# The adaLN matmuls of layer 0 with the weights as the stationary side, and a copy of scan states on VectorE

## The chip, the cores and the metric

The kernel runs on one core of a Trainium2 chip. The metric is the device time of one launch in microseconds, as the median of several runs. In the text PE is TensorE (the matmuls), DVE is VectorE, ACT is ScalarE, POOL is GpSimd, and SP is the engine whose queue issues most of the DMA transfers.

## The reference

One inference step of a hybrid backbone with two layers. 128 prompt tokens and 1024 latent tokens, 1152 in all, have 1024 channels. Each layer normalizes x, modulates it, feeds the result `h` to three branches (an S5 state-space scan, a Fourier mixing, an attention), gates and merges them, and adds the result to x. Cut to what matters here:

```python
def adaln(cvec, w, b):                       # w: (1024, 3072), b: (3072,)
    m = jax.nn.silu(cvec) @ w + b
    shift, scale, gate = jnp.split(m[:, None, :], 3, axis=-1)
    return shift, scale, gate

# in mixer_layer, with cvec = c_ctx for the prompt and c for the latents:
    shift, scale, gate = adaln(cvec, ada_w, ada_b)
    h = rmsnorm(x, norm_g) * (1.0 + scale) + shift
    a_in, a_gate, f_in, f_gate, q, k, v, c_gate = jnp.split(h @ w_in, SPLITS, axis=-1)
    # S5: hs[t] = a_bar * hs[t-1] + b_bar @ u[t], forwards and backwards;
    # the prompt's final states of both directions are an output (new_state_ssm)
```

There are thus only two conditioning vectors, and the product `silu(cvec) @ w` has two rows. All is computed in fp32.

## The kernel before

The channels lie on the 128 partitions in 8 blocks (`KD`), the 1152 tokens in the free dimension, in three groups j = 0, 1, 2 of 384. The dense products (`dense`, line 269) hold a 128x128 block of the weights as the stationary side and 384 tokens as the moving side. Weights and `h` are split in a rounded part and a rest (`whi`, `wlo`; `hh`, `hl`), and three matmuls give one product. ACT rounds the weights, POOL subtracts, and ACT mostly evicts a finished block from PSUM (`jo`) with two buffers `pd` in turn.

The head of the program, in `run` (line 1541), comes ahead of layer 0:

- `setup` (line 176) loads the identity, the first x tile, the small vectors (`fvst`, 128 rows of 128 numbers) and constants on SP's queue, transposes the vectors on PE into columns (`fv`) and computes the silu of both conditioning vectors (`silc`).
- `x_gen` (line 398) takes nine x tiles of 128 tokens: ACT and DVE sum the squares, PE transposes eight blocks of 128x128, ACT and DVE evict them into `A1` (in the profile `A`).
- `ada_gen` (line 306) computes the shift and scale of layer 0. The conditioning columns are the stationary side (4 columns), the weights move, 512 columns at a time. 16 units of 512 KB are loaded with `ada_load` into four buffers `aw`. Of each unit one half goes as an fp32 matmul, the other is rounded on ACT, subtracted on DVE or POOL and goes as two matmuls. After four units a row of results (`adarow`) is copied by ACT and turned into columns by four matmuls with `sel` as the moving side (`ada_row`).
- `rb_first_gen` computes the row scales of all tokens (DVE, a power on POOL, transposes on PE, a copy by ACT) and x times the scale for j = 0 (`xr0`). `h_first_gen` makes `h` for three j and first k from 0 to 3, then from 4 to 7, with `h_unit` (line 456): one product, an addition on ACT (`hh`), a difference on DVE (`hl`); j = 0 needs them twice, since prompt and latents have different shifts and scales.

In each layer, `scan_gen` (line 706) runs 128 steps of the scan on DVE, four operations each, beside 12 dense blocks. In the first 16 steps it also advances the prompt's states; these steps end with the prompt's final states in column 16 of `H` (in the profile `A`). When the scan has been traced, `finals` (line 727) copies them (`ss_fin`, on ACT), transposes them on PE, copies the results on ACT into a tile of tag `qk_sq` and stores them. Behind the scan the q/k/v work goes on beside two dense blocks; then the pool `gp` of this stage is closed and the next one, with `ssm_out_gen` (line 738, it reads the scanned states), opens.

The order of the instructions of an engine isn't the order of the program. The framework plans it when the program is built, from its own estimates of when an instruction's inputs are ready, and program order as the priority. On the chip each engine then works off its list strictly in that order, and waits at an instruction whose inputs are late, whatever stands behind it. DMA queues are issued in the same way.

Of the kernel before, what the change touches and what calls it, by code (L numbers as in the profile page):

```python
# [9 lines left out]
F = mybir.dt.float32  # L10
R = mybir.dt.float32r
AF = mybir.ActivationFunctionType
OP = mybir.AluOpType
# [10 lines left out]
KD = D // 128  # L24
# [77 lines left out]
class Program:  # L102
# [73 lines left out]
    def setup(self):  # L176
        nc, I = self.nc, self.I
        self.ident = self.sb("ident", [128, 128])
        self.dma(self.ident, I["ident"])
        self.load_x(0, 1)  # L180
        self.identr = self.sb("identr", [128, 128], R)
        nc.gpsimd.dma_start(self.identr, I["ident"])
        self.ones = self.sb("ones", [128, 1])
        nc.vector.memset(self.ones, 1.0)
        self.fold = self.sb("fold", [128, 32])
        for i in range(4):
            nc.vector.tensor_copy(self.fold[32 * i:32 * i + 32], self.ident[32 * i:32 * i + 32, 32 * i:32 * i + 32])
        self.half9 = self.sb("half", [128, 9])
        nc.gpsimd.memset(self.half9, -0.5)
        self.half = self.half9[:, :8]  # L190
        vecs = [("c", I["c"][0], 8), ("c_ctx", I["c_ctx"], 8), ("norm_g", I["norm_g"], 16), ("ada_b", I["ada_b"], 48),
                ("merge_b", I["merge_b"], 48)]
        st = self.sb("fvst", [128, 128], pool=self.xp)
        off = 0
        self.fv = {}
        col = self.sb("fv", [128, 128])
        for nm, ap, k in vecs:
            self.dma(st[off:off + k], ap.rearrange("l (k p) -> (l k) p" if len(ap.shape) == 2 else "(k p) -> k p", p=128))
            n = k // DEPTH
            for l in range(1 if len(ap.shape) == 1 else DEPTH):  # L200
                self.fv[nm, l] = col[:, off + n * l:off + n * l + (n if len(ap.shape) == 2 else k)]
            off += k
        ps = self.pst("pv")
        self.tr(ps[:, :off], st[:off])
        self.act(col[:, :off], ps[:, :off])
        self.mods = {}
        self.sel = self.sb("sel", [4, 2])
        self.dma(self.sel, I["sel"])
        self.silc = self.sb("silc", [128, KD, 4])
        nc.gpsimd.memset(self.silc, 0.0)  # L210
        sc = self.silc[:, :, 0:2]
        self.act(sc[:, :, 0], self.fv["c_ctx", 0], AF.Silu)
        self.act(sc[:, :, 1], self.fv["c", 0], AF.Silu)
        self.sc4 = self.sb("sc4", [128, KD, 4], R)
        self.act(self.sc4[:, :, 0:2], sc)
        self.tt(self.sc4[:, :, 2:4], sc, self.sc4[:, :, 0:2].bitcast(F), OP.subtract)
        self.hmb = []
        for l in range(DEPTH):
            t = self.sb(f"hmb{l}", [128, 24])
            nc.vector.tensor_scalar(t, self.fv["merge_b", l], 0.5, None, op0=OP.mult)  # L220
            self.hmb.append(t)
        self.dmask = self.sb("dmask", [128, 16])
        self.dma(self.dmask, I["dmask"])
        self.xT_d = [self.dp.tile([D, NT], F, name=f"xTd{l}") for l in range(DEPTH)]

    def vec_cols(self, v):
# [76 lines left out]
        self.dma(st, self.I["ada_w"][l, 256 * k:256 * k + 256, 512 * o:512 * o + 512].rearrange("(a p) n -> p a n", p=128))  # L303
        return st

    def ada_gen(self, l, pool, parts, bufs=3, first=False):
        self.ada_alloc(l)
        units = [(o, k) for o in parts for k in range(4)]
        ld = {}
        def load(i):  # L310
            ld[i] = self.ada_load(l, pool, bufs, *units[i])
        for i in range(bufs - 1):
            load(i)
        for i, (o, k) in enumerate(units):
            if i + bufs - 1 < len(units):
                load(i + bufs - 1)
            if i == 0:
                pa = self.ps.tile([128, 3, 512], F, name="pa", tag="pa", bufs=1)
            ps = pa[:, i // 4 % 3]
            st = ld.pop(i)  # L320
            for h in range(2):
                ends = (k == 0 and h == 0, k == 3 and h == 1)
                if first and (h == 0 or i >= 16):
                    self.mm(ps[0:4, :], self.silc[:, 2 * k + h], st[:, h], *ends)
                else:
                    w = self.sb("awr", [128, 2, 512], R, bufs=3 if first else 2, pool=pool)
                    self.act(w[:, 0], st[:, h])
                    self.tt(w[:, 1], st[:, h], w[:, 0].bitcast(F), OP.subtract, e=self.nc.gpsimd if first and i >= 7 else None)
                    self.mm(ps[0:4, :], self.sc4[:, 2 * k + h], w[:, 0], ends[0], False)
                    self.mm(ps[0:4, :], self.sc4[:, 2 * k + h], w[:, 1], False, ends[1])  # L330
                if h == 0:
                    if i > 3 and k == 0:
                        self.ada_row(l, units[i - 1][0], row)
                    yield 2 * 216
            if k == 3:
                row = self.sb("adarow", [4, 512], bufs=1, pool=pool)
                self.act(row, ps[0:4, :])
            if i + 1 == len(units):
                self.ada_row(l, o, row)
            yield 2 * 216  # L340

    def ada_row(self, l, o, row):
        pc = self.pst("pt")
        for b in range(4):
            self.mm(pc[:, 2 * b:2 * b + 2], row[:, 128 * b:128 * b + 128], self.sel)
        self.ada_out(l, o, pc)

    def ada_out(self, l, o, pc):
        mod, A = self.mods[l]["mod"], self.mods[l]["A"]
# [127 lines left out]
                self.h_unit(l, j, k, xT[:, k, 384 * j:384 * j + 384], rb, self.xr_tile())  # L477
                yield 900

    def rb_first_gen(self, xT, ssq):  # L480
        self.tt(ssq[:, 0], ssq[:, 0], ssq[:, 1], OP.add)
        r = self.rstd_cols(ssq[:, 0], 9)
        self.rb = [self.rstd_rows(r[:, 3 * j:3 * j + 3], 3) for j in range(3)]
        self.h_tiles()
        self.xr0 = self.sb("xr0", [128, KD, 384], pool=self.xp)
        for k in range(KD):
            self.tt(self.xr0[:, k], xT[:, k, 0:384], self.rb[0], OP.mult)
            yield 500

    def h_first_gen(self, xT, js, ks):  # L490
        for j in js:
            for k in ks:
                if j == 0:
                    self.h_unit(0, j, k, self.xr0[:, k], None, self.xr_tile())
                else:
                    self.h_unit(0, j, k, xT[:, k, 384 * j:384 * j + 384], self.rb[j], self.xr_tile())
                yield 500

    def rhs_h(self, k, j):
        return self.hh[j][:, k], self.hl[j][:, k]  # L500
# [205 lines left out]
    def scan_gen(self, l):  # L706
        S, H = self.S, self.H
        for k in range(128):
# [13 lines left out]
            self.tt(t1, t1, nxt, OP.add)  # L722
            self.tt(nxt, t1, t2, OP.add)
            yield 800
        self.finals(l)

    def finals(self, l):
        H = self.H
        fin = self.sb("ss_fin", [128, 2, 32], pool=self.gp)
        self.act(fin, H[:, :, :, 16])  # L730
        o = self.sb("qk_sq", [32, 2, 64, 2], pool=self.gp)
        for r in range(2):
            ps = self.pst("pv")
            self.tr(ps[:32, :128], fin[:, r])
            self.act(o[:, :, :, r], ps[:32, :128].rearrange("g (d n) -> g d n", d=2))
        self.dma(self.O[4][0, l].rearrange("d g n r -> g d n r"), o)
# [552 lines left out]
    def layer(self, l, cs):  # L1289
# [140 lines left out]
        with self.spool:  # L1430
# [11 lines left out]
            with self.pool("qp", l):  # L1442
                with self.pool("gp", l, "q"):
                    self.qkt = self.qkv_tables(l)
                    def qkv():
                        yield from self.qkv_gen(l, qs_d, k_d, v_d, (0,))
                        yield from self.qkv_gen(l, qs_d, k_d, v_d, (1,))
                    q = qkv()
                    self.run_some(q, 8)
                    drive((self.scan_gen(l), 103), (self.dense(12), 140))  # L1450
                    drive((q, 78), (self.dense(2), 21))
                with self.pool("gp", l, "o"):
                    drive((self.dense(6), 12*6), (self.ssm_out_gen(l, a_d, y_d), 33), (self.qtail_gen(), QT))
        with self.pool("gp", l, "u"):
# [86 lines left out]
    def run(self):  # L1541
        self.open_ssm(0)
        with ExitStack() as cs:
            self.np_ = cs.enter_context(self.tc.tile_pool(name="np", bufs=1))
            self.xp = cs.enter_context(self.tc.tile_pool(name="xp", bufs=1))
            self.setup()
            self.load_x(1, 9)
            self.xT0 = xT = self.sb("A1", [128, KD, NT])
            ssq = self.sb("ssqt", [128, 2, 9], pool=self.xp)
            ada = self.ada_gen(0, self.xp, (2, 0, 3, 1), 4, True)  # L1550
            next(ada)
            self.run_all(self.x_gen(xT, ssq))
            rb = self.rb_first_gen(xT, ssq)
            head = self.h_first_gen(xT, [0, 1, 2], range(0, 4))
            for i, _ in enumerate(ada):
                if i >= 10:
                    self.run_some(rb if i < 18 else head, 1)
            self.run_all(rb)
            self.run_all(head)
            self.run_all(self.h_first_gen(xT, [0, 1, 2], range(4, 8)))  # L1560
        for l in range(DEPTH):
            for j in range(3):
                self.debug(f"hh{l}", self.hh[j].bitcast(F), (slice(None), slice(None), slice(384 * j, 384 * j + 384)))
# [31 lines left out]
```

## Time and profile before

| | us |
|---|---|
| median of 3 runs | 2754.29 (2752.75 to 2756.11) |
| the profiled execution's own time | 2752.03 |
| its span in the profile | 2750.3 |
| PE busy | 2627.0 (96%) |
| DVE busy | 1826.6 (66%) |
| ACT busy | 1143.5 (42%) |
| POOL busy | 683.4 (25%) |

The span is the time from the first to the last instruction of the profiled execution. Busy times are sums over the instructions of an engine; PE's ends of matmuls are modelled, so that neighbouring matmuls overlap in the rows. Times in rows count from the span's start. PEclk is the granted clock of TensorE, 1.00 for 2.4 GHz and 0.50 for 1.2 GHz.

### The profile page before, as it was taken

The page shows a single profiled execution, that of the slowest core. Times are in us where ns is not written, and L with a number is a line of the kernel's source. Part 1 is how long each engine was busy: PE and PEld are TensorE (multiplying, and loading weights), DVE is VectorE, ACT ScalarE, POOL GpSimd, SP SyncE. Part 2 cuts the span into 40 slices and gives each one's busy share as a digit, 9 for nine tenths or more (in the row PEclk, how much of TensorE's full clock was granted, in tenths as well). Part 3 has the DMA queues.
Part 4 walks back from the last instruction along what each step waited for, and adds up shares of the span by engine and source line. Part 5 has one row for each costly group of instructions (what it writes and reads, how often), then busy time and mean ns, then how long its engine had stood idle before and what let it go on. Part 6 is the DMA issues. An engine that isn't in the chain of part 4 may idle for free. (4 is left out here: it accounts for less than half of the span.)

```text
span 2750.3 us, 44553 instructions
## 1 busy us (share of the span) xinstructions
PE 2627.0 (96%) x16092; PEld 2509.0 (91%) x16092; DVE 1826.6 (66%) x3933; ACT 1143.5 (42%) x2676; POOL 683.4 (25%) x521
## 2 busy tenths in 40 slices
PE   7998999899999999999999899999999999999998
PEld 3898999799999999999989899989989998999998
DVE  6549955856558889866572797577654788891343
ACT  5461145331355565423345322543223655553244
POOL 3241122322321020132343212233222202102223
PEclk9999999999999999999999999999999999999999
DMA  6632223566263345544543222345645334433244
GB/s 223 178 99 84 95 87 110 150 191 207 86 202 114 110 138 153 173 126 114 165 146 93 95 89 84 107 125 160 211 154 174 109 121 150 143 121 98 80 121 149
DMA packets 459997, 366.85 MB, mean 133 GB/s; under 512 B 72953, under 2 KB 432001, under 8 KB 459777
## 3 DMA queue, kind: packets, MB, share of 16 engines
q1 hardware_dynamic: 458480, 359.75, 42.9%
q0 software_dynamic: 1296, 4.26, 0.5%
q8 instruction: 127, 2.08, 0.3%
q14 instruction: 94, 0.76, 0.1%
HBM read 243.52 MB, written 120.39 MB: 132 GB/s over the span
## 5 line engine op out<-in xcount | busy, mean ns | idle before, releaser
L168 PE MATMUL pd<-hh,whi 128*128 128x384 f32 x2496 | 857.1, 344 | 24.0 <-ACT jo L142 20.1
L168 PE MATMUL pd<-hh,wlo 128*128 128x384 f32 x2496 | 844.6, 339 | 3.2 <-POOL wlo L145 3.2
L168 PE MATMUL pd<-hl,whi 128*128 128x384 f32 x2496 | 843.1, 338 | 1.3 <-DVE hl L149 1.3
L145 POOL TENSOR_TENSOR wlo<-wst,whi 128x512 fp32r<-128x512 f32 x312 | 437.9, 1405 | 1525.8 <-ACT whi L142 1404.8
L168 PEld LDWEIGHTS pd<-hh,whi 128*128 128x128 f32 x2496 | 472.5, 189 | 35.0 <-ACT jo L142 22.8
L168 PEld LDWEIGHTS pd<-hh,wlo 128*128 128x128 f32 x2496 | 472.5, 189 | 7.8 <-POOL wlo L145 5.7
L168 PEld LDWEIGHTS pd<-hl,whi 128*128 128x128 f32 x2496 | 473.1, 190 | 3.8 <-DVE hl L149 2.3
L168 PE MATMUL pd<-A,whi 128*128 128x384 f32 x1728 | 458.2, 342 | 8.2 <-ACT jo L142 4.9
L168 PEld LDWEIGHTS pd<-A,whi 128*128 128x128 f32 x1728 | 311.2, 189 | 11.7 <-ACT jo L142 5.6
L142 ACT ACTIVATE whi<-wst 128x512 fp32r<-128x512 f32 x312 | 196.0, 630 | 278.5 <-PE pd L168 190.6
L168 PE MATMUL pd<-A,wlo 128*128 128x384 f32 x864 | 293.9, 340 | 0.0
L1078 DVE TENSOR_REDUCE at_mx<-pa 128x1 f32<-128x1152 f32 x128 | 173.3, 1354 | 16.1 <-PE pa L168 15.7
L168 PE MATMUL pa<-at_K,at_Q 128*128 128x384 f32 x768 | 167.2, 347 | 8.6 <-ACT at_P L142 5.8
L142 ACT ACTIVATE at_PT<-pt 128x384 fp32r<-128x384 f32 (+1 forms) x260 | 114.9, 490 | 144.0 <-PE pt L173 143.6
L142 ACT ACTIVATE at_P<-pa,at_mx 128x1152 f32<-128x1152 f32 x128 | 158.1, 1235 | 20.7 <-DVE at_mx L1078 19.4
L168 PEld LDWEIGHTS pd<-A,wlo 128*128 128x128 f32 x864 | 163.2, 189 | 0.1
L168 PEld LDWEIGHTS pa<-at_K,at_Q 128*128 128x128 f32 x768 | 128.3, 188 | 29.0 <-ACT at_P L142 25.5
L168 PE MATMUL pt<-qkW,hh 128*128 128x384 f32 x576 | 150.7, 343 | 0.0
L168 PE MATMUL pv<-at_PT,at_V 128*128 128x256 f32 x1152 | 148.8, 283 | 0.0
L168 PEld LDWEIGHTS pv<-at_PT,at_V 128*128 128x128 f32 x1152 | 144.7, 191 | 0.8
L142 ACT ACTIVATE jo<-pd 128x384 f32<-128x384 f32 x120 | 58.0, 485 | 198.1 <-PE pd L168 96.5
L145 DVE TENSOR_TENSOR at_PT<-pt,at_PT 128x384 fp32r<-128x384 f32 (+1 forms) x260 | 133.1, 550 | 10.0 <-ACT at_PT L142 7.8
(294 smaller groups left out, 3772.3 us busy)
## 6 DMA issues: line engine op xcount, KB each, us to landing
aw<-in_ada_w_dram SPq DMA_DIRECT2D x48, 512.0 KB, 4.8
wst<-in_merge_w_dram SPq DMA_DIRECT2D x96, 256.0 KB, 3.0
wst<-in_w_in_dram SPq DMA_DIRECT2D x80, 256.0 KB, 2.9
td<-jo SPq DMA_DIRECT2D x96, 192.0 KB, 2.3
jt<-td SPq DMA_DIRECT2D x96, 192.0 KB, 2.8
wst<-in_w_out_dram SPq DMA_DIRECT2D x64, 256.0 KB, 2.9
sgd<-jo SPq DMA_DIRECT2D x72, 192.0 KB, 2.0
jt<-sgd SPq DMA_DIRECT2D x64, 192.0 KB, 2.7
```

Of the source, the lines that this page charges most:

```text
L142: return self.nc.scalar.activation(out, in_, func, **kw)
L145: return (e or self.nc.vector).tensor_tensor(out=out, in0=a, in1=b, op=op)
L168: return self.nc.tensor.matmul(out, w, x, start=first, stop=last, **kw)
L1078: nc.vector.tensor_reduce(out=mx[:, 0:1], in_=src, axis=AX.XY if m3 else AX.X, op=OP.max, negate=True)
```

## The change

Two edits. In the head, the adaLN weights of layer 0 become the stationary side: `ada_first_gen` loads 8 units, each 256 columns of the weights over all 1024 rows, in two transfers of 512 KB into four buffers, and multiplies each 128x128 block with the two conditioning columns. The result is in columns at once. The units come in pairs, the scale and the shift of the same two blocks k. x tiles 3 to 8 are loaded between the first units and transposed between the pairs; row scales are computed for each j alone; `h` of j = 0 is made for two k after each pair, that of j = 1 one pair later, that of j = 2 at the end. The small vectors and two constants are loaded on POOL's queue. `ada_gen`, `ada_row`, `sel` and the split copy `sc4` go; `ada_out` stays for the other parts of adaLN.

In each layer, `finals` is called after the q/k/v work, and its first copy goes to DVE. `keep_in_program_order` makes the planner keep it behind every instruction traced before it on DVE.

```diff
 def setup(self):
-        self.load_x(0, 1)
-        self.identr = self.sb("identr", [128, 128], R)
-        nc.gpsimd.dma_start(self.identr, I["ident"])
+        self.load_x(0, 3)
+        pdma = nc.gpsimd.dma_start
...
-            self.dma(st[off:off + k], ap.rearrange("l (k p) -> (l k) p" if len(ap.shape) == 2 else "(k p) -> k p", p=128))
+            pdma(st[off:off + k], ap.rearrange("l (k p) -> (l k) p" if len(ap.shape) == 2 else "(k p) -> k p", p=128))
...
-        self.dma(self.dmask, I["dmask"])
+        pdma(self.dmask, I["dmask"])
+        self.identr = self.sb("identr", [128, 128], R)
+        pdma(self.identr, I["ident"])
...
+    def ada_first_gen(self, l, pool):
         self.ada_alloc(l)
...
+        mod, A = self.mods[l]["mod"], self.mods[l]["A"]
+        units = [2 * q + 8 * p for q in range(4) for p in (1, 0)]
+        ld = []
+
+        def load(m):
+            st = self.sb("aw", [128, KD, 256], bufs=4, pool=pool)
             for h in range(2):
+                self.dma(st[:, 4 * h:4 * h + 4], self.I["ada_w"][l, 512 * h:512 * h + 512, 128 * m:128 * m + 256].rearrange("(k p) n -> p k n", p=128))
+            ld.append(st)
+
+        for i in range(4):
+            load(units[i])
+            self.load_x(3 + i, 4 + i if i < 3 else 9)
+        pa = self.ps.tile([128, 3, 512], F, name="pa", tag="pa", bufs=1)
+        for i, m in enumerate(units):
+            ps = pa[:, i % 3, 0:4].rearrange("p (m c) -> p m c", c=2)
+            for b in range(2):
+                for k in range(KD):
+                    self.mm(ps[:, b], ld[i][:, k, 128 * b:128 * b + 128], self.silc[:, k], k == 0, k == KD - 1)
+            if i < 4:
+                load(units[i + 4])
+            s = slice(m, m + 2)
+            self.tt(mod[:, s], ps, self.fv["ada_b", l][:, s][:, :, None].to_broadcast([128, 2, 2]), OP.add)
+            if m >= 8:
+                g = slice(m - 8, m - 6)
+                self.stt(A[:, g], mod[:, s], 1.0, self.fv["norm_g", l][:, g][:, :, None].to_broadcast([128, 2, 2]), OP.add, OP.mult)
+            yield i
...
+    def rb_first(self, ssq, j):
+        c = slice(3 * j, 3 * j + 3)
+        self.tt(ssq[:, 0, c], ssq[:, 0, c], ssq[:, 1, c], OP.add)
+        self.rb[j] = self.rstd_rows(self.rstd_cols(ssq[:, 0, c], 3), 3)
...
 scan_gen:
             yield 800
-        self.finals(l)
...
 finals:
-        self.act(fin, H[:, :, :, 16])
+        self.tc.keep_in_program_order(self.nc.vector.tensor_copy(fin, H[:, :, :, 16]))
...
 layer:
                     drive((q, 78), (self.dense(2), 21))
+                    self.finals(l)
...
 run:
+            ada = self.ada_first_gen(0, self.xp)
+            xg = self.x_gen(xT, ssq)
+            self.run_some(xg, 6)
+            self.h_tiles((0,))
+            self.rb_first(ssq, 0)
+            for q in range(4):
+                self.run_some(ada, 2)
+                for k in (2 * q, 2 * q + 1):
+                    self.xr_first(xT, k)
+                    self.h_first(xT, 0, k)
+                if q < 3:
+                    self.run_some(xg, 4)
+                if q == 1:
+                    self.h_tiles((1,))
+                    self.rb_first(ssq, 1)
+                if q == 2:
+                    self.run_all(xg)
+                    self.h_tiles((2,))
+                    self.rb_first(ssq, 2)
+                if q > 0:
+                    for k in (2 * q - 2, 2 * q - 1):
+                        self.h_first(xT, 1, k)
+            for k in (6, 7):
+                self.h_first(xT, 1, k)
+            for k in range(KD):
+                self.h_first(xT, 2, k)
```

`xr_first` and `h_first` hold the bodies of the former loops: x times the row scale for j = 0, and one call of `h_unit`.

## Rows read from the trace of the kernel before

**Rows 1.** The page: the span, part 1, and one group of part 5.

```profile
span 2750.3 us, 44553 instructions
PE 2627.0 (96%) x16092; PEld 2509.0 (91%) x16092; DVE 1826.6 (66%) x3933; ACT 1143.5 (42%) x2676; POOL 683.4 (25%) x521
...
L168 PE MATMUL pd<-hh,whi 128*128 128x384 f32 x2496 | 857.1, 344 | 24.0 <-ACT jo L142 20.1
```

**Rows 2.** Windows of all engines: x tiles, adaLN, first dense blocks.

```profile
core 0: us, PE busy (x) PEld busy (x) DVE busy (x) ACT busy (x) POOL busy (x), PEclk, DMA share, GB/s
8.25:14.15 5.90, 4.09 (x17) 3.35 (x17) 1.85 (x9) 4.90 (x12) 0.00 (x0) 1.00 0.82 292
14.15:24.50 10.35, 8.79 (x56) 6.52 (x56) 7.34 (x22) 9.95 (x23) 0.00 (x0) 1.00 1.04 403
24.50:65.10 40.60, 32.90 (x98) 8.04 (x98) 28.31 (x51) 19.90 (x40) 20.98 (x13) 0.83 0.62 197
65.10:100.00 34.90, 32.52 (x176) 29.25 (x176) 26.49 (x77) 19.12 (x45) 6.48 (x5) 1.00 0.65 183
```

**Rows 3.** Timeline of PE in the head: start, duration, group, idle time before it.

```profile
8.48 1.94 PE L173 MATMUL pt<-ident,hl 128*128 128x128 f32 x8 [8.48 <-DMA dmask<-in_k_dmask_dram]
...
52.80 0.59 PE L168 MATMUL pa<-awr,sc 128*4 128x512 f32 x1 [3.60 <-POOL awr L145]
...
65.16 0.34 PE L168 MATMUL pd<-hh,whi 128*128 128x384 f32 x1
```

**Rows 4.** Timeline of ACT in the scan stage, layer 0 and layer 1.

```profile
223.66 0.32 ACT L142 ACTIVATE ss_fin<-A 128x64 f32<-128x64 f32 x1 [12.25 <-DVE A L145]
...
1565.48 0.32 ACT L142 ACTIVATE ss_fin<-A 128x64 f32<-128x64 f32 x1 [12.25 <-DVE A L145]
```

**Rows 5.** Timeline of PE, the first dense matmul behind each of those copies.

```profile
224.93 0.69 PE L168 MATMUL pd<-hh,whi 128*128 128x384 f32 x1 [7.84 <-ACT jo L142]
...
1566.74 0.69 PE L168 MATMUL pd<-hh,whi 128*128 128x384 f32 x1 [7.83 <-ACT jo L142]
```

**Rows 6.** Windows of all engines after those two matmuls, and just behind.

```profile
224.93:240.00 15.07, 15.07 (x72) 15.07 (x73) 14.24 (x49) 2.46 (x5) 3.48 (x3) 0.81 0.31 99
240.00:255.07 15.07, 15.07 (x89) 15.07 (x88) 14.18 (x53) 3.12 (x6) 2.72 (x2) 1.00 0.29 94
1566.74:1580.00 13.26, 13.26 (x63) 13.26 (x64) 12.57 (x43) 2.47 (x5) 3.52 (x3) 0.80 0.28 90
1580.00:1593.26 13.26, 13.26 (x78) 13.26 (x78) 12.50 (x45) 2.63 (x5) 2.78 (x2) 1.00 0.30 96
```

**Rows 7.** Timeline of DVE, its first instruction after the scan of layer 0.

```profile
369.01 0.17 DVE L871 TENSOR_SCALAR qk_ss<-qk_ss 128x4 f32<-128x4 f32 x1 [10.85 <-ACT qk_j L142]
```

**Rows 8.** DMA issues: queue, count, KB each, median us from issue to landing.

```profile
aw<-in_ada_w_dram SPq DMA_DIRECT2D x48, 512.0 KB, 4.8
...
fn_t<-in_k_dft_l_dram POOLq DMA_DIRECT2D x8, 512.0 KB, 8.1
```

**Rows 9.** PE windows of four sel matmuls: length, busy (x), PEclk, DMA share, GB/s.

```profile
32.57:33.55 0.98, 0.98 (x9) 1.00 0.88 328
55.86:57.65 1.79, 1.79 (x9) 0.50 1.12 330
```

**Rows 10.** Timeline of PE, the sums of squares of layer 1.

```profile
1370.14 0.72 PE L168 MATMUL pv<-ones,ssq 128*128 128x1 f32 x6
```

**Rows 11.** Windows of all engines, 50 to 60 us.

```profile
50.00:55.00 5.00, 1.53 (x3) 0.17 (x3) 2.08 (x5) 1.87 (x5) 3.97 (x2) 0.50 0.13 32
55.00:60.00 5.00, 5.00 (x14) 1.96 (x12) 2.41 (x7) 2.57 (x6) 2.79 (x3) 0.50 1.01 283
```

**Rows 12.** The instructions of tile fn_t: POOL's DMA issues, ns min/median/max.

```profile
L993 POOL DMA_DIRECT2D fn_t<-in_k_dft_l_dram x8: 537/545/647, 670.6 to 2013.1; - x8
```

**Rows 13.** Timeline of DVE and of POOL in the head.

```profile
36.57 8.16 DVE L145 TENSOR_TENSOR xr<-A,rb 128x384 f32<-128x384 f32 x8 [1.46 <-ACT rb L142]
...
25.54 2.13 POOL L145 TENSOR_TENSOR rs<-ms,half 128x9 f32<-128x9 f32 x1 [23.36 <-DVE ms L432]
```

More of the change, by code (lines that the diff above doesn't have):

```diff
@@ L206, in setup @@
         self.mods = {}
[L207 to L211, printed above, removed]
+        self.silc = self.sb("silc", [128, KD, 2])
+        sc = self.silc
         self.act(sc[:, :, 0], self.fv["c_ctx", 0], AF.Silu)
         self.act(sc[:, :, 1], self.fv["c", 0], AF.Silu)
-        self.sc4 = self.sb("sc4", [128, KD, 4], R)
-        self.act(self.sc4[:, :, 0:2], sc)
-        self.tt(self.sc4[:, :, 2:4], sc, self.sc4[:, :, 0:2].bitcast(F), OP.subtract)
         self.hmb = []
@@ L304, in ada_load @@
         return st
-    def ada_gen(self, l, pool, parts, bufs=3, first=False):
+    def ada_first_gen(self, l, pool):
         self.ada_alloc(l)
[L308 to L320, printed above, removed]
-            for h in range(2):
[L322 to L346, printed above, removed]
+        mod, A = self.mods[l]["mod"], self.mods[l]["A"]
[3 more added lines that the diff above has]
+            st = self.sb("aw", [128, KD, 256], bufs=4, pool=pool)
+            for h in range(2):
+                self.dma(st[:, 4 * h:4 * h + 4], self.I["ada_w"][l, 512 * h:512 * h + 512, 128 * m:128 * m + 256].rearrange("(k p) n -> p k n", p=128))
+            ld.append(st)
@@ L478, in h_gen, with xr_first, h_first @@
                 yield 900
[L480 to L497, printed above, removed]
+    def rb_first(self, ssq, j):
+        c = slice(3 * j, 3 * j + 3)
+        self.tt(ssq[:, 0, c], ssq[:, 0, c], ssq[:, 1, c], OP.add)
+        self.rb[j] = self.rstd_rows(self.rstd_cols(ssq[:, 0, c], 3), 3)
+    def xr_first(self, xT, k):
+        self.tt(self.xr0[:, k], xT[:, k, 0:384], self.rb[0], OP.mult)
+    def h_first(self, xT, j, k):
+        if j == 0:
+            self.h_unit(0, j, k, self.xr0[:, k], None, self.xr_tile())
+        else:
+            self.h_unit(0, j, k, xT[:, k, 384 * j:384 * j + 384], self.rb[j], self.xr_tile())
     def rhs_h(self, k, j):
@@ L1546, in run @@
             self.setup()
-            self.load_x(1, 9)
             self.xT0 = xT = self.sb("A1", [128, KD, NT])
             ssq = self.sb("ssqt", [128, 2, 9], pool=self.xp)
[L1550 to L1560, printed above, removed]
+            self.rb = {}
+            self.xr0 = self.sb("xr0", [128, KD, 384], pool=self.xp)
+            ada = self.ada_first_gen(0, self.xp)
[24 more added lines that the diff above has]
+                self.h_first(xT, 2, k)
         for l in range(DEPTH):
```

## The prediction

> **What bounds the kernel now.** First the page: its span is 2750.3 us, PE is busy for 96% of it and no other engine for more than 66% [rows 1]. So a change pays only where it closes a gap of PE, or lets PE run at its higher clock. The list of the costliest groups then shows which gaps: the largest group of dense matmuls has 24.0 us of idle time before it, and 20.1 of that ended when ACT wrote a `jo` [rows 1]. These two views give two places: the scan stage of each layer, and the head, which the windows by stage show to be 65.1 us long before the first dense matmul.
>
> In the head [rows 2] the x tiles are transposed until 24.5; DMA moves 403 GB/s then. From 24.5 to 65.1 PE counts 32.90 of 40.60 us busy at a mean granted clock of 0.83, and DMA moves only 197 GB/s. So in the adaLN stage the transfers aren't the bound: the loads wait for buffers, and these for the matmuls. PE itself waits for rounding and subtraction on ACT and POOL (3.60 us for POOL before 52.80), and the first dense matmul starts at 65.16 [rows 3].
>
> In the scan stage ACT's instruction list holds the copy of the final states `ss_fin` at 223.66 and 1565.48, in both layers after an idle time of 12.25 us that the scan on DVE ended [rows 4]. Behind it stands the eviction of a finished dense block; PE waits for that 7.84 and 7.83 us [rows 5], and comes back at a lower clock.
>
> **Part 1, the copy.** The copy leaves ACT, so the wait for the scan leaves ACT's list. Two PE gaps go: 7.84 + 7.83 = 15.7 us. After them PE issued 72 matmuls in 15.07 us where the next 15.07 us hold 89, and 63 in 13.26 us where the next hold 78 [rows 6]: 17/89 x 15.07 = 2.9 and 15/78 x 13.26 = 2.5 us lost to the clock. Together 21.1 us, the upper bound. What is late next? With PE 10.7 us further on, DVE's first work after the scan, which now comes after 10.85 us of idle time [rows 7] (the same in layer 1), arrives just as the scan ends. So this cover is used up within 0.2 us, and I take 20 us. The copy itself goes to DVE, 0.32 us on ACT before [rows 4], behind everything that was traced there up to the end of the q/k/v work. Two transposes, two copies on ACT and the store of the states follow it; they existed before. They now stand at the boundary to the stage that reads the scanned states, where the next tiles want the memory of this stage's. Lower bound: if that stage's start slips in each layer by what a transfer takes to land, 4.8 us for the adaLN loads [rows 8], 20 - 9.6 = 10 us stay.
>
> **Part 2, the adaLN matmuls.** Removed: 16 loads of 512 KB, 16 fp32 matmuls with 512 moving columns, 16 pairs of rounded ones, 16 roundings on ACT, 16 subtractions on DVE and POOL, four row copies and 16 small matmuls with `sel`. Added: 8 units of 1 MB in two transfers each, so the same bytes; and 8 x 16 = 128 fp32 matmuls, each with a 128x128 block of the weights as the stationary side and two moving columns. The trace of before has no such matmul with 128 rows, but two near ones: four `sel` matmuls (128 stationary columns, two moving) fill the window 32.57 to 33.55, so 0.245 us each [rows 9]; three with 128x128 stationary and one moving column, two records for each matmul, take 0.72 us, 0.24 each [rows 10]. And the same four `sel` matmuls fill 55.86 to 57.65 where the granted clock is 0.50: 0.448 us each [rows 9]. So the 128 cost 31.4 us at the high level (2.4 GHz) and 57.3 us at the low one (1.2 GHz). Which?
>
> The clock stood at 0.50 through 50 to 55, after a stretch in which PE was mostly idle, and still through 55 to 60, although PE is counted busy for 5.00 of these 5 us [rows 11]; over a third of that was the group of `sel` matmuls. With 512 moving columns PE kept the high level from 24.5 until it idled. I read this as: a stretch of such small matmuls is counted busy by the view, and the clock treats it more like an idle one. No row shows 7 us of nothing else, which a pair of units would be. I take the low level for most of the changed head, as 55 to 60 is the nearest row, and keep the high level as the other bound.
>
> [...]
>
> The head at the low level, from the first transpose at 8.48, which waits for the first x tile as before: eight transposes took 1.94 us [rows 3], so 24 take 5.8 (to 14.3). The vectors now come over POOL's queue; its issues cost 0.545 us each [rows 12], and its 512 KB transfers took 8.1 us to land [rows 8]; seven small ones are issued within about 5 us of the start and land near 13 at worst. With the silu chain and the power on POOL (2.13 us, [rows 13]) I let the first unit start at 16.7. Then 57.3 for the units, 48 transposes at 0.24 (11.5), and 9 of the row scales (2.2): 87.7. After each pair of x tiles the clock may return for a few us; I take three times 2.3 us off, my choice between none and six: 80.7. The dense part then begins at the low level and loses what it lost after the two stalls, 2.7 us, and about 1.3 us to late `hh` and `hl`: 84.7. Before, the like point is 65.2 plus the 2.4 us that PE idles in 65.1 to 100 [rows 2] plus 1.0 for the last `sel` group: 68.6. Head: +16, bounds +10 (clock back more often) and +23 (never).
>
> What hides the rest: the transfers, nine x tiles of 0.52 MB and 8.4 MB of weights, need 32.5 us at the 403 GB/s of [rows 2], so they end before PE does even if shorter rows cost a third. DVE's products of x and the row scales (8.16 us, [rows 13]) and all of `h` for j = 0 lie under the units. DVE has time for j = 1 too; what is left after the last unit is two of eight k.
>
> **The sum.** 20 gained, 16 lost: -4. The profiled execution took 2752.03 us beside its span of 2750.3, the median of the runs is 2754.29. So 2748 by the former, 2750 by the median, which I forecast.
>
> **Rivals.** (a) *The small matmuls keep the high level.* For it: the group of 0.98 us ran at 1.00 [rows 9], and weight loads would fill PE all through. Against it: 55 to 60. Then the head is 16.7 + 31.4, six tiles at 10.35 us for 56 transposes, 1.48 a tile (8.9), and nine row scales (1.2): 58.2, plus 1.3: 59.5 against 68.6, -9; with the copy's -20 it gives 2725. (b) *In-order lists couple x tiles to h.* If ACT's and DVE's evictions of x tiles stand behind the h of a pair, PE's transposes wait for a chain of some 4 us (two products of 1.02, six small operations of 0.3) in each of four quarters, up to +14 on top of +16, so 2764: slower. It decides from a head that ends 26 us later than now, the copy's 20 and the 5.5 below. For it: lists are planned on estimates, and `ss_fin` shows one planned wrong. Against it: these evictions are ready early, and PE has other work. (c) *The copy's gain is eaten at the stage's end*, as bounded above: 10 instead of 20 with the slow head, 2760.
>
> **How the numbers follow.** Forecast case 0.50, its own range 2743 to 2760 (head +10 to +23, copy 17 to 21); (a) 0.35, 2719 to 2731; (b) and (c) 0.15. The range to hold 8 in 10 takes most of (a) and reaches into (b): 2720 to 2760. This kernel can tell about 0.2%, 5.5 us, from no change. Faster than 2748.8: all of (a) and 0.4 of the forecast case, 0.55. Slower than 2759.8: three quarters of (b) and (c) and 0.08 of the forecast case, 0.15. The rest, 0.30, is no change.
>
> **What would show it.** Right: no `ss_fin` on ACT, dense blocks without a break through the scan's first steps at clock 1.00, both layers; a DVE idle time after the scan near zero; units of 16 matmuls at some 7 us and a clock of 0.50 between 20 and 80; the first dense matmul near 81. Wrong: units of 3.9 us at 1.00 with the first dense matmul before 60 (then (a)); PE idle before transposes for ACT or DVE in the head (then (b)); a longer gap than now before the Toeplitz matmuls after the q/k/v work (then (c)).

## The result, and the profile after

The changed kernel is slower. Four runs of each side gave 2769.61 us against 2753.64: a ratio of 1.0056 (1.0039 to 1.0074), +15 us. A second measurement (the run after_again below) gave 1.0063 (1.0049 to 1.0078), +17 us. The forecast was 2750 with a range of 2720 to 2760. The profiled execution took 2766.33 us beside its span of 2764.6, so +14.3 in the span.

The page after, lines that answer to [rows 1]:

```profile
span 2764.6 us, 44817 instructions
...
PE 2649.6 (96%) x16252; PEld 2558.4 (93%) x16252; DVE 1823.3 (66%) x3937; ACT 1129.4 (41%) x2653; POOL 666.9 (24%) x519
...
L168 PE MATMUL pd<-hh,whi 128*128 128x384 f32 x2496 | 861.9, 345 | 9.2 <-ACT jo L142 5.3
```

The wait for a `jo` of ACT went from 20.1 to 5.3 us: the copy's half of the change does what it says. PE is still 96% busy, and it is busy for 23 us longer. Timeline of PE in the head, for [rows 3], and windows of all engines, for [rows 2, 11]:

```profile
10.13 0.66 PE L173 MATMUL pt<-ident,hl 128*128 128x128 f32 x2 [10.13 <-DMA hl<-in_x_prompt_dram]
11.90 0.45 PE L173 MATMUL pv<-ident,fvst 128*128 128x128 f32 x1 [1.11 <-DMA fvst<-in_merge_b_dram]
...
17.32 5.62 PE L168 MATMUL pa<-silc,aw 128*128 128x2 f32 x32
...
42.03 6.83 PE L168 MATMUL pa<-silc,aw 128*128 128x2 f32 x32
...
52.03 0.87 PE L173 MATMUL pt<-ident,rs 128*128 128x128 f32 x3 [1.37 <-ACT A L142]
...
55.66 1.21 PE L168 MATMUL pa<-silc,aw 128*128 128x2 f32 x8
...
57.09 2.83 PE L168 MATMUL pa<-silc,aw 128*128 128x2 f32 x24
61.67 0.90 PE L173 MATMUL pt<-ident,rs 128*128 128x128 f32 x3 [1.76 <-POOL rs L145]
...
69.45 6.99 PE L168 MATMUL pa<-silc,aw 128*128 128x2 f32 x32 [0.26 <-DVE mod L145]
...
83.53 0.67 PE L168 MATMUL pd<-hh,whi 128*128 128x384 f32 x1
```

```profile
core 0: us, PE busy (x) PEld busy (x) DVE busy (x) ACT busy (x) POOL busy (x), PEclk, DMA share, GB/s
10.13:17.32 7.19, 5.13 (x26) 3.98 (x26) 2.77 (x11) 5.59 (x13) 0.00 (x0) 1.00 1.10 356
17.32:83.53 66.21, 62.57 (x315) 61.21 (x314) 28.17 (x83) 17.53 (x40) 4.02 (x4) 0.54 0.49 162
42.03:48.86 6.83, 6.83 (x34) 6.83 (x34) 1.01 (x5) 0.00 (x0) 0.85 (x1) 0.50 0.43 148
55.66:59.92 4.26, 4.25 (x36) 4.17 (x35) 1.85 (x5) 1.04 (x3) 0.00 (x0) 0.90 0.37 88
57.09:59.60 2.51, 2.51 (x26) 2.51 (x24) 0.69 (x1) 0.00 (x0) 0.00 (x0) 1.00 0.04 10
69.45:76.44 6.99, 6.98 (x32) 6.89 (x32) 2.56 (x6) 1.97 (x5) 0.00 (x0) 0.50 0.00 0
```

A unit is 32 records, two for each of 16 matmuls. One execution shows it at both levels of the clock: 6.83 us at 0.50, and 1.21 + 2.83 = 4.04 us in the window of 0.90. Of that unit the last 24 records, 12 matmuls in 2.83 us, lie but for their end in the stretch at 1.00, so 0.24 us a matmul there against 0.43 at 0.50. PE is counted busy for 62.57 of the 66.21 us, and the mean granted clock is 0.54. In 69.45 to 76.44 no transfer moves any more and no other engine is busy for half the time: there these matmuls alone set the pace. The first dense matmul comes at 83.53 instead of 65.16.

Then the scan and its end. DVE's first instruction after the scan, for [rows 7], the copy and what follows it in both layers, and PE at the same places:

```profile
377.69 0.17 DVE L848 TENSOR_SCALAR qk_ss<-qk_ss 128x4 f32<-128x4 f32 x1
...
489.93 0.21 DVE L707 COPY ss_fin<-A 128x64 f32<-128x64 f32 x1
493.20 0.69 DVE L145 TENSOR_TENSOR ss_CA<-ss_EC,ss_Cre 128x512 f32<-128x512 f32 x1 [3.07 <-issue]
...
1830.82 0.21 DVE L707 COPY ss_fin<-A 128x64 f32<-128x64 f32 x1
1834.11 1.52 DVE L145 TENSOR_TENSOR ss_CA<-ss_EC,ss_Cre 128x512 f32<-128x512 f32 x1 [3.08 <-DMA out_dram<-qk_sq]
```

```profile
490.19 0.28 PE L173 MATMUL pv<-ident,ss_fin 128*32 128x128 f32 x1 [1.16 <-DVE ss_fin L707]
...
1831.09 0.28 PE L173 MATMUL pv<-ident,ss_fin 128*32 128x128 f32 x1 [1.17 <-DVE ss_fin L707]
```

The idle time of 10.85 us after the scan is gone. In its place stands a new one: `ss_CA`, the first tile of the next stage, waits 3.1 us in each layer, and in layer 1 the releaser is named: the store of the states out of `qk_sq`. PE waits 1.2 us for the copy ahead of its transposes. The stretches of [rows 6] that showed a clock below 1.00, now some 17 us later, keep the high clock in both layers:

```profile
242.50:257.57 15.07, 15.07 (x88) 15.07 (x87) 14.31 (x45) 3.63 (x7) 4.63 (x4) 1.00 0.28 88
...
1583.44:1596.70 13.26, 13.26 (x78) 13.26 (x77) 12.51 (x42) 2.79 (x6) 3.18 (x3) 1.00 0.26 84
```

### The profile page after: what moved, and what is told of

Same layout as the page of the kernel before. It is cut to its first block, busy times and chain, and to the rows that moved or that the text cites. A ratio compares the mean times of both kernels' runs of the same rounds, so it can differ in the third digit from the quotient of the medians.

```text
span 2764.6 us, 44817 instructions
## 1 busy us (share of the span) xinstructions
PE 2649.6 (96%) x16252; PEld 2558.4 (93%) x16252; DVE 1823.3 (66%) x3937; ACT 1129.4 (41%) x2653; POOL 666.9 (24%) x519
## 4 chain that ended last, share of the span: by engine, by line
PE 61%; DVE 8%; DMA 5%; ACT 3%; issue 3%; POOL 1%; SPq 0%; DVEq 0%; POOLq 0%; ACTq 0%
PE pd L168 41%; PE pa L168 6%; PE pv L168 5%; PE pt L168 4%; PE pt L173 3%; PE pv L173 1%; DVE jo L145 1%; DVE jo L149 1%; DVE at_P L1059 1%; ACT at_P L142 1%; DVE xr L149 1%; DMA aw<-in_ada_w_dram 1%; DVE aacc L149 1%; DMA jo<-zbd 1%; ACT A L142 1%
```

## The experiments

Each ratio is against the kernel before, run on the same chip in the same rounds; us are that ratio times some 2754.

**The two parts alone.** copy_only is the kernel before with the second part; head_only is the changed kernel without it.

```diff
 copy_only, in finals and in the layer:
-        self.act(fin, H[:, :, :, 16])
+        self.tc.keep_in_program_order(self.nc.vector.tensor_copy(fin, H[:, :, :, 16]))
...
                     drive((q, 78), (self.dense(2), 21))
+                    self.finals(l)
 head_only: these lines as before, all others as after
```

> The kernel before with the second part of the change alone: ss_fin copied by DVE, traced after the q/k/v work; the head is that of before. Theory A (the recorded sum was right for this part): about -20 us, 2734. Theory B (in the trace of the changed kernel the scan stage gained 8.9 and 10.5 us, from the offsets of the first qk_ss against those of the stage's start, +17.6 to +8.7 and +16.7 to +6.4, and 2.1 and 3.2 us of it went again up to the first Toeplitz tile): about -14 us, 2740, and the losses behind that come from the head's part. Theory C (the copy's move also causes the 7.5 us that were lost between the attention of layer 0 and the start of layer 1): -5 to -8 us, 2747.

> The kernel before with the first part of the change alone: the adaLN units, their loads, and h pair by pair; ss_fin stays on ACT inside the scan. With theories A and B: the head costs what the first dense matmul shows, 83.53 against 65.16, so +18 us, 2772, or up to +25 (2779) if the later losses belong to it. If the copy's wait on ACT costs less here than in the kernel before, the scan stage gives some of it back: then below +15.

copy_only: 0.9964 (0.9952 to 0.9975), -10 us. head_only: 1.0126 (1.0106 to 1.0145), +35. So theory A falls: the copy is worth half of the 20 us. Against the kernel before, the last `qk_qo` of the two layers comes 11.4 and 16.7 us earlier, the first Toeplitz tile only 6.6 and 12.5: 4.8 and 4.2 us go at the stage's end. Theory B was right about the place and too hopeful by 4 us. Theory C's -8 lies inside the interval (-13 to -7) too, but what it says does not happen: copy_only is 5.6 us ahead at the first `at_mx` of layer 0 and 5.0 at the start of layer 1's scan. The head costs more than its first dense matmul shows (83.14 in this trace, +18). The trace of copy_only, DVE at both stage ends, against the same place in the kernel before (second fence), where `ss_CA` followed the last product of q/k/v without a pause:

```profile
472.57 0.20 DVE L729 COPY ss_fin<-A 128x64 f32<-128x64 f32 x1
475.82 0.69 DVE L145 TENSOR_TENSOR ss_CA<-ss_EC,ss_Cre 128x512 f32<-128x512 f32 x1 [3.04 <-issue]
...
1811.98 1.61 DVE L145 TENSOR_TENSOR ss_CA<-ss_EC,ss_Cre 128x512 f32<-128x512 f32 x1 [3.54 <-DMA out_dram<-qk_sq]
```

```profile
481.95 0.56 DVE L145 TENSOR_TENSOR qk_qt<-qk_qr,qk_qt 128x384 fp32r<-128x384 f32 x1 [0.59 <-ACT qk_qt L142]
482.56 0.68 DVE L145 TENSOR_TENSOR ss_CA<-ss_EC,ss_Cre 128x512 f32<-128x512 f32 x1
```

**Is it the store's memory?** copy_far is copy_only with another tile for the stored states.

```diff
-        o = self.sb("qk_sq", [32, 2, 64, 2], pool=self.gp)
+        o = self.jo()[0:32, 0:256].rearrange("g (d n r) -> g d n r", d=2, n=64)
```

> The kernel before with the second part of the change alone, as in the run copy_only, but the tile from which the states are stored is one of the jo buffers instead of one in this stage's memory. Theory (rival (c) of the prediction: the next stage's first tile waits for the memory that the store still reads): the 3.04 us of idle time on DVE before the first ss_CA go to near zero in both layers, 2735 to 2737 against copy_only's 2741.7. Rival (the boundary's loss is PE's and DVE's wait for the copy itself, or a later wait takes its place): 2740 to 2743.

0.9934 (0.9919 to 0.9949), -18 us, where copy_only had -10. DVE in layer 0 and layer 1:

```profile
472.96 0.68 DVE L145 TENSOR_TENSOR ss_CA<-ss_EC,ss_Cre 128x512 f32<-128x512 f32 x1 [1.38 <-issue]
...
1802.45 0.68 DVE L145 TENSOR_TENSOR ss_CA<-ss_EC,ss_Cre 128x512 f32<-128x512 f32 x1 [1.39 <-issue]
```

The wait shrank from 3.04 and 3.54 to 1.4 us rather than to zero; the rest falls on the transposes of `ss_fin`, which stay in this stage's memory (in wide_far below, where `ss_fin` lies elsewhere, DVE has no idle time there). The two waits shrank by 3.8 us together, and the time by some 8; the two intervals leave room for either. With the store out of the way the copy brings nearly the 20 us of the prediction.

**Is it the clock?** head_wide gives the adaLN matmuls 128 moving columns; head_half leaves half of them out.

```diff
 head_wide (pw: a view of pa, 128 columns a product, of which ps is the first):
-  self.mm(ps[:, b], ld[i][:, k, 128 * b:128 * b + 128], self.silc[:, k], k == 0, k == KD - 1)
+  self.mm(pw[:, b, :, 0:64], ld[i][:, k, 128 * b:128 * b + 128], self.silc[:, k, :, None].to_broadcast([128, 2, 64]), k == 0, k == KD - 1)
 head_half:
-                for k in range(KD):
+                for k in range(KD // 2):
```

> The changed kernel, in which the 128 adaLN matmuls have 128 moving columns (each of the two vectors repeated 64 times by a stride of zero) instead of 2; only the first column of each is read. Theory (the granted clock falls because the engine streams next to nothing, though it is counted busy): the clock stays at 1.00 in the head, a unit of 16 takes 4 to 7 us, the first dense matmul comes at 60 to 75 instead of 83.5, and the kernel takes 2745 to 2760. Rival (the clock falls for the stretches of waiting before the units, or for the weight loads themselves): 0.50 as in the changed kernel, a unit takes 8 us or more, 2775 or more.

> The changed kernel without the second half of the contraction of the layer-0 modulation: 64 of the 128 adaLN matmuls are left out, all transfers stay. If PE's small matmuls at the low level set the head: 64 x 0.427 = 27 us less, first dense matmul near 56, 2742. Rival (behind them the h on DVE or the transfers set the head): 5 to 15 us less, 2755 to 2765.

head_wide: 0.9970 (0.9959 to 0.9980), -8 us, so some 24 us less than the changed kernel. PE's timeline and two windows of it:

```profile
45.23 3.84 PE L169 MATMUL pa<-silc,aw 128*128 128x128 f32 x32
49.45 3.74 PE L169 MATMUL pa<-silc,aw 128*128 128x128 f32 x32
52.94 0.42 PE L169 MATMUL pd<-hh,whi 128*128 128x384 f32 x1
53.44 3.84 PE L169 MATMUL pa<-silc,aw 128*128 128x128 f32 x32
```

```profile
25.00:30.00 5.00, 5.00 (x46) 4.91 (x45) 4.42 (x13) 2.24 (x8) 0.00 (x0) 1.00 1.06 388
...
50.00:55.00 5.00, 5.00 (x45) 4.78 (x44) 3.68 (x9) 2.86 (x7) 3.10 (x3) 1.00 0.11 28
```

The clock stays at 1.00 through the units, and a unit with 64 times the moving columns takes 3.84 us instead of 6.83. The unit came out a little shorter than the 4 to 7 us expected, and the first dense matmul at 52.94, ahead of the last unit, instead of 60 to 75. Both kernels load the same weights in the same order; the moving columns differ, with them the granted clock, and the planner spreads the transposes of x more finely among the first units. So the slow units were slow by the clock, and the rival, that the waits ahead of the units or the loads themselves bring it down, falls. What is late next is `h`: DVE is busy for 5.00 of 5.00 us from 60 to 70. head_half: 0.9972 (0.9960 to 0.9984), 2746 us where 2742 was expected, first dense matmul at 59.91. PE's timeline:

```profile
33.60 3.41 PE L168 MATMUL pa<-silc,aw 128*128 128x2 f32 x16
...
43.74 1.84 PE L168 MATMUL pa<-silc,aw 128*128 128x2 f32 x16
...
49.86 3.41 PE L168 MATMUL pa<-silc,aw 128*128 128x2 f32 x16
...
59.91 0.69 PE L168 MATMUL pd<-hh,whi 128*128 128x384 f32 x1 [2.81 <-ACT whi L142]
```

64 matmuls fewer move the first dense matmul by 83.53 - 59.91 = 23.6 us, 0.37 each, between the 0.24 and 0.43 of the two levels. Half a unit takes 1.84 us or 3.41, so 0.23 or 0.43 a matmul. A caution on reading: the windows put 1.00 beside the unit at 33.60, but the first clock event of this trace lies behind 43 us, and ahead of it that number is no reading. (The same holds for most of the window 10.13 to 17.32 of the changed kernel above, whose first event lies at 15.2.) Units of the same length stand at 0.50 where the clock is read.

**The missing 13 us: the tiles' places?** The head alone costs +35, and 18 of it is seen at the first dense matmul. From 124 us of the kernel before on, every engine has the same instructions in the same order in head_only as there. But the changed kernel's setup tiles are smaller, and the tiles allocated behind them (x^T, `h`, the dense weights, `jo`) lie elsewhere, 32 bytes off modulo 64. Four kernels move tiles and, but for one memset, do nothing else; "after_place" and "head_place" put them at the addresses of the kernel before.

```diff
 before_shift, behind sel:       + self.pad = self.sb("pad", [128, 8]);  nc.vector.memset(self.pad, 0.0)
 after_pad, behind silc:         + self.pad = self.sb("pad", [128, 24]); nc.vector.memset(self.pad, 0.0)
 after_place and head_place:     + self.pad = self.sb("pad", [128, 56]); nc.vector.memset(self.pad, 0.0)
                                 + self.ada_alloc(0) behind the allocation of A1; rb_first ahead of h_tiles
```

> The kernel before with one unused tile of 32 bytes a partition behind sel, which moves all later tiles by 32 bytes and changes nothing else. Theory (place): interval 174.4 ns instead of 173.3, about +12 us, 2765. Rival: no change, 2753.

> The changed kernel with one unused tile of 96 bytes a partition, allocated behind silc, which puts every tile that is allocated behind it back to the place modulo 128 bytes that it had before the change (the changed kernel's smaller setup tiles had moved them by 32 modulo 64). Theory (place): in pure dense stretches a matmul of 384 columns started each 174.44 ns in the three kernels with the new head and each 173.33 ns in the two with the old one; some 10,900 such matmuls at 1.11 ns are 12 us, so this kernel takes about 2757, and the interval goes back to 173.3. Rival (the slower pace has to do with the new head itself, or the loss behind it is chance of single executions): the interval stays at 174.4 and the time near 2769.

> The changed kernel unchanged, for more runs on the same chip as these. If the parts add up: head at the first dense matmul +18, place +12, copy -10: +20; the first measurement was +15.5 (10.7 to 20.4).

> The changed kernel with an unused tile of 224 bytes and two allocations traced in another order, so that x, h, the dense weights and all later long-lived tiles lie at the very addresses that they have in the kernel before. In the run before_shift a move of 32 bytes alone brought the mean start-to-start interval of dense matmuls from 174.06 to 174.56 ns and the time by +1.4 us (-1 to +4); after_pad, at other addresses again, had 175.33 and +21. Theory (place, some 5 us of the changed kernel's loss: 10,900 matmuls at 0.5 ns): interval 174.1, about +11 to +12 against before, 2766. Rival (place costs nothing here): +16 to +17.

Measured: before_shift 1.0005 (0.9996 to 1.0015), after_pad 1.0076 (1.0063 to 1.0090), after_again 1.0063 (1.0049 to 1.0078), after_place 1.0052 (1.0033 to 1.0070). The pace does depend on the place. ACT's evictions of a pure dense stretch in layer 1, twelve blocks of 24 matmuls apart, of before, before_shift and after_pad:

```profile
1603.13 0.47 ACT L142 ACTIVATE jo<-pd 128x384 f32<-128x384 f32 x1
...
1653.05 0.47 ACT L142 ACTIVATE jo<-pd 128x384 f32<-128x384 f32 x1
```

```profile
1604.96 0.48 ACT L142 ACTIVATE jo<-pd 128x384 f32<-128x384 f32 x1
...
1655.20 0.47 ACT L142 ACTIVATE jo<-pd 128x384 f32<-128x384 f32 x1
```

```profile
1603.15 0.49 ACT L142 ACTIVATE jo<-pd 128x384 f32<-128x384 f32 x1 [3.38 <-issue]
...
1653.71 0.49 ACT L142 ACTIVATE jo<-pd 128x384 f32<-128x384 f32 x1 [3.37 <-issue]
```

That is 49.92, 50.24 and 50.56 us for 288 matmuls: 173.3, 174.4 and 175.6 ns each. At the old addresses after_place is back at 49.92. But the time does not follow as I had reckoned: 12 us were expected of the shift and +1.4 (-1 to +4) came, and after_pad, which was to win 12, came out 4 above after_again (the intervals overlap). Over all matmuls of 384 columns behind the head the mean start-to-start differs by only 0.5 ns (174.06 and 174.56, from some 10,900 starts each), not 1.1, since those on `A` keep their pace; that bounds the place at an estimated 5 us of the change, and after_place (+14, 9 to 19) can't tell 5 from nothing.

**Or a late start as such?** head_only was run again, head_place takes the place out of it, and before_late delays the old head by 80 dependent copies of the identity matrix on ACT.

```diff
 before_late:
+        late = [self.sb(f"late{i}", [128, 128], pool=self.xp) for i in range(2)]
-        self.dma(self.ident, I["ident"])
+        self.dma(late[0], I["ident"])
+        for i in range(80):
+            self.act(late[(i + 1) % 2], late[i % 2])
+        self.act(self.ident, late[0])
```

> The run head_only once more: it gave +34.7 (29 to 40) from 4 executions, where the first dense matmul came 18 us late and the changed kernel with the copy's -10 was at +16 to +17. If the parts add up: +27. If it stays at +35, the copy's move is worth 18 to 19 us with the new head and 10 with the old.

> The run head_only at the addresses of the kernel before. Behind the head the instructions stand in the same order on every engine as in the kernel before, and now at the same addresses. Theory (place makes the excess): +18 to +22. Rival (the excess has another cause): +30 or more.

> The kernel before with 80 dependent copies of the identity matrix on ACT ahead of the first transpose, some 20 us; nothing else. Theory (a delay of the head costs what the first dense matmul shows): the time rises by as much as the first dense matmul is later, within 4 us. Rival (a later start of the layers costs more than itself): at least 8 us more than that.

head_only_again: 1.0115 (1.0097 to 1.0132), +32. head_place: 1.0103 (1.0087 to 1.0120), +28. before_late: 1.0107 (1.0093 to 1.0122), +29. The delay is read at the scan rather than at the first dense matmul, which in before_late came ahead of the last adaLN units, only 12.6 us late; by the yardstick put on record its rival would have held. First line of the tile `ss_s`, of before, before_late, head_place and head_wide (first and last start behind the durations):

```profile
L145 DVE TENSOR_TENSOR ss_s<-ss_AR,A x128: 273/280/1381, 190.0 to 357.2; 128x64 f32<-128x64 f32 x112, 128x128 f32<-128x128 f32 x16
```

```profile
L145 DVE TENSOR_TENSOR ss_s<-ss_AR,A x128: 273/279/1383, 217.4 to 384.5; 128x64 f32<-128x64 f32 x112, 128x128 f32<-128x128 f32 x16
```

```profile
L145 DVE TENSOR_TENSOR ss_s<-ss_AR,A x128: 272/279/1369, 209.4 to 376.5; 128x64 f32<-128x64 f32 x112, 128x128 f32<-128x128 f32 x16
```

```profile
L146 DVE TENSOR_TENSOR ss_s<-ss_AR,A x128: 272/280/1393, 183.4 to 353.0; 128x64 f32<-128x64 f32 x112, 128x128 f32<-128x128 f32 x16
```

before_late starts its scan 27.4 us late and ends 29 (26 to 34) late: a late start costs itself and, as far as the interval can tell, no more. head_place starts it 19.4 late and ends 28 (24 to 33) late, between its theory and its rival. So with the place and the late start taken out, some 9 us (5 to 14) of the new head's cost arise behind the scan's start, and no run here says why. Three readings narrow it. It seems not to hang on the slow units: head_wide keeps the high clock and starts the scan 6.6 us earlier than before, which with the copy's -10 would make -17, and it measures -8 (-11 to -5.5); wide_place below, at the old addresses, has -12 where it would be -17, and there the intervals still touch. In single traces head_place's lag grows from 19.4 us at the scan to 27.1 at the end of the span, but before_late's grows too, from 27.4 to 31.4, so only some 4 of the 8 us are the new head's own there. And it is idle time of PE rather than a slower clock: from the first dense matmul to the end, before and head_place have the same granted clock, and PE is idle for 104.0 and 113.6 us.

```profile
65.16:2750.30 2685.14, 2581.12 (x15923) 2491.11 (x15921) 1788.19 (x3846) 1107.45 (x2604) 661.23 (x502) 0.99 0.43 131
```

```profile
85.44:2777.40 2691.96, 2578.34 (x15915) 2489.59 (x15915) 1787.46 (x3835) 1106.34 (x2602) 662.02 (x503) 0.99 0.43 131
```

Part of it is seen in the attention stage of layer 0: from the first to the last `at_mx` the five traces with the old head take 353.9 to 355.1 us, the twelve with the new one 356.2 to 360.9.

**Versions that the runs point to.** wide_place is head_wide at the old addresses. wide_far also keeps `ss_fin` in memory that outlives the stage, and traces its transposes and store behind the next stage; after_far is after_place with that.

```diff
-        fin = self.sb("ss_fin", [128, 2, 32], pool=self.gp)
+        self.fin = fin = self.sb("ss_fin", [128, 2, 32], pool=self.qp)
...
+    def finals_store(self, l):
+        fin = self.fin
+        o = self.jo()[0:32, 0:256].rearrange("g (d n r) -> g d n r", d=2, n=64)
...
                     drive((self.dense(6), 12*6), (self.ssm_out_gen(l, a_d, y_d), 33), (self.qtail_gen(), QT))
+                    self.finals_store(l)
```

> The run head_wide (128 moving columns) with the addresses of the kernel before, as in after_place. Head_wide had -8.2 (-11 to -5.5). Theory (place): some 5 us less, -13. Rival: -8.

> The version that the runs point to: wide_place, with ss_fin in memory that outlives the stage, its transposes, copies and store traced behind the work of the next stage, and stored from a jo buffer. With copy_far against copy_only (-18.2 against -9.9) and the 1.5 us of PE idle and 1.4 us of DVE idle in each layer that copy_far still had before the transposes and the first ss_CA: 8 to 13 us less than wide_place, so -18 to -26, 2730 to 2737.

> The run after_place (+14.3) with ss_fin in memory that outlives the stage and its transposes, copies and store behind the next stage's work, as in wide_far. If the stage's end costs the same behind the new head (copy_far against copy_only 8.3 us, wide_far against wide_place 8.8): +5 to +7.

wide_place: 0.9958 (0.9944 to 0.9973), -12; its interval overlaps head_wide's -8, so the place is not resolved here either. wide_far: 0.9926 (0.9911 to 0.9941), -20, the lowest of all and some 36 us ahead of the changed kernel. But copy_far, with the old head, has -18 (-22 to -14): even at the high clock no gain of the new head over the old one is shown. after_far: 1.0043 (1.0028 to 1.0059), +12 where +5 to +7 was expected. Its first Toeplitz tile does stand 4.8 us earlier than after_place's in layer 0, but the last `at_mx` of that layer comes 2.2 us later: the attention stage took back much of what the stage end gave. The two intervals overlap, so the gain behind the slow head stays unproven.

## Why the prediction was wrong, step by step

**What bounds the kernel** was right: both places were gaps of PE or stretches at the low clock, and both moved the time.

**The copy: this step failed.** Everything up to the end of q/k/v came as written: no `ss_fin` on ACT, dense blocks through the scan's first steps at 1.00, no idle time on DVE after the scan. Those gave 11 to 12 us in each layer in copy_only, a little over the 10.6 of the sum. The error is the term "I take 20 us", near the upper end of its own bounds. The lower bound, 4.8 us a layer at the stage boundary, was what happened: 4.8 and 4.2 us, and -10 us (-13 to -7) in all. That its size fits so well is luck: it was priced by the landing of a 512 KB load, while the store in copy_only lands 1.7 us after its issue, and the copy, the transposes and ACT's copies ahead of it make up the rest of DVE's wait. The reason was in the text ("the next tiles want the memory of this stage's") and was kept as rival (c) rather than in the sum. copy_far shows it: with another memory the wait for the store is gone, and the time is -18. What could have been read ahead: before the change DVE goes from the last `qk_qt` to `ss_CA` without a pause (the fence behind copy_only), so anything put between them that ends in a transfer had no cover there.

**The adaLN units** were priced well. Forecast 0.245 us a matmul at the high level and 0.448 at the low one; measured 0.23 to 0.24 and 0.43. The low level for most of the head was right, the clock came back for one unit of eight (and part of the first, 5.62 us) instead of "three times 2.3 us", the first unit began at 17.32 (16.7), and the first dense matmul came at 83.53 ("near 81"). At that point the head costs 18.4 us against the +16 of the sum, and 16.7 to 19.6 at the scan's start in the eight traces with these units, within the bounds of +10 to +23. Two slips in that sum change nothing: 87.7 less three times 2.3 is 80.8, and the bound with six returns is +9. The Trainium skill (TensorE: Matmul & The Clock Gate, LDWEIGHTS (loading the stationary operand)) gives a weight load as its columns divided by 1.2, in ns, and names no clock beside it; with two loads for each fp32 matmul, a unit is by it an estimate of 3.4 us. The trace comes near it at 1.00 (16 x 0.23 = 3.7) and not at 0.50 (6.83).

**What the new head costs behind its units: this step failed too.** The sum let the head's cost end with the first dense matmuls (2.7 us at the low clock, 1.3 for late `hh` and `hl`) and put everything behind them at nothing, without a reason. head_only stands at +32 to +35 and head_place at +28 (24 to 33), outside the bound of +23; that is some 13 us above the first dense matmul in head_only. Three suspects were looked at: the place of the tiles, estimated at some 5 us and not resolved by the times; the late start, which shows no cost beyond itself; and the clock behind the head, which is the same. Some 9 us (5 to 14) stay open; they are idle time of PE, and their cause isn't known. Of the 20 us between the forecast of -4 and the measured +15 to +17, the copy timed alone makes 10, and this remainder most of the rest. Also open: the parts don't quite add up. -10 and +33 make +23, and the change is +15 to +17, so behind the new head the copy is worth some 16 us rather than 10, with intervals of 3 to 5 us on each.

**The rivals.** (a) fell: the units' clock did not hold. head_wide, where it holds, shows what it would have been worth: the scan starts 6.6 us earlier, near the -9 of (a), but the kernel has -8 where (a), with 20 us for the copy, had -29. (b) fell: behind the first unit PE waits twice ahead of transposes, 1.37 and 1.76 us, where (b) had some 4 us in each of four quarters. (c) held, in both layers. With the forecast's own head it had been put at 2760; the open remainder took it to 2770.

## What to carry to other kernels

Taking a wait out of one engine's list is worth what the next wait leaves of it: follow the moved step to its last transfer, and ask which tile of the next stage takes that memory; storing from memory that outlives the stage was worth some 8 us here in two pairs of runs, and 2 (not proven) behind the slow head. PE can be counted busy all through and still be granted the low clock, as in these units with two moving columns; here a wider moving side cost nothing (3.84 against 6.83 us a unit) and kept the high one. A part that looks settled at its own end can still cost more later: time each change to the end of the kernel as well. When a difference of 0.2% is to be explained, time each part of the change alone, and compare the addresses of the tiles too.

## What the runs showed of the hardware

An fp32 matmul with a 128x128 stationary block took 0.43 us with 2 moving columns at the granted clock of 0.50 (16 in 6.83 us), 0.23 us with 2 at 1.00 (8 in 1.84 us, head_half), and 0.24 us with 128 at 1.00 (16 in 3.84 us). Moving every long-lived tile by 32 bytes lengthened 288 dense matmuls of 384 columns from 49.92 to 50.24 us, and another placement (after_pad, moved from the old one by a multiple of 128 bytes) to 50.56; the total followed by +1.4 us (-1 to +4) in the first case. The same program's executions differ by more than such effects: from the first dense matmul to the end of the span one trace of the changed kernel took 2681.1 us and another 2689.6.
